# Routing each head in its own span of gather slots, five w_q kept for both tiles, nine row buffers and a 4 KB descriptor ring

## The chip, the cores and the metric

One core of one Trainium2 chip runs the whole program. The metric is the device time of one execution in microseconds; 1544.36 us is the median of three runs of the kernel before.

## The reference

A decoder trunk of two layers over 256 tokens with 1024 channels, all in float32. Each layer mixes tokens with four parallel head groups and then applies a PEER feed-forward, which looks up experts by product keys:

```python
for l in range(DEPTH):                                    # DEPTH = 2
    proj = x @ w_in[l]                                    # 1024 -> 2208 columns
    mix  = concat[short conv, MLA, conformer conv, windowed attention](proj)
    mix  = rms_norm per 64-channel head
    h    = layer_norm(ALPHA * x + mix @ w_out[l])
    x    = layer_norm(ALPHA * h + peer_ffn(h))

def chunk(xc):                                            # 128 tokens
    q  = (xc @ w_q).reshape(c, 8 heads, 2, 128)
    sc = einsum(q, sub_keys)                              # 2 x 128 scores a head
    top_s, top_i = top_k(sc, 16)                          # of each half
    best = top_k(sums of all 16 x 16 pairs, 16)           # 16 experts a head
    u, v = u_tab[idx], v_tab[idx]                         # 8 x 16 rows of 1024 each
    act  = gelu(einsum(u, xc))
    return einsum(softmax gate * act, v)
```

So each token reads 128 rows of u and of v per layer, and these rows are most of the traffic.

## The kernel before

The 256 tokens are two tiles of 128 (t = 0, 1), one token to a partition. With two layers there are four pairs (l, t), worked through in the order (0,0), (0,1), (1,0), (1,1).

**The gather loop.** `peer(l, t, h, acc)` makes 128 slots per pair, 512 in all. One slot is: an indirect DMA issued by POOL (L756) brings one expert's u and v for each of 128 tokens into a buffer `row` (128 x 2048 float32, 1.05 MB); DVE multiplies the u half by h and sums it (L759); ACT makes the gelu, the gate and a diagonal matrix `dg` (L741, L742, L744); PE adds `dg` times the v half into two PSUM banks `acc` (L746). The pool `gp` has `ROWS` = 10 buffers `row`, so a gather can be issued when PE has finished with the gather ten slots earlier.

**The routing.** `route(l, hd, hTs)` gives the indices of one head: it loads the head's weights `w_q` (1.18 MB, `load_w` on SP's queue), makes q and the scores on PE (L675, L680), and finds the two top-16 lists and the expert numbers on DVE (L632 to L658). With both tiles in `hTs` it serves both from one load. Heads 0 to 4 (`HS` = 5) are routed tile by tile, in `solo`; heads 5 to 7 for both tiles together, in `joint`. Of the first five, heads 0, 1 and 2 (`HELD`) keep `w_q` in buffers of their own (pool `rp`) until the second tile has used it; heads 3 and 4 load it a second time. Other weights (`w_in` pieces, `w_out`, remaining `w_q`) share three buffers `w` (pool `wp`).

**The mixer.** `mixer(l, t, ...)` makes h of a pair: nine pieces of `w_in`, two attentions, two convolutions, then `outs`, which multiplies by four loads of `w_out` (L586), one for each head group. h of (0,0) must be ready before the first gather; the other three mixers run beside the gathers of the pair before them.

**The order of work.** Routing and mixers are Python generators that yield a cost now and then. `paced(gather, tasks)` emits one slot of gathers, then advances each task `(generator, a, b, cost)` so that it is done evenly between slots a and b. Dependencies without semaphores (`keep_behind`) hold this work near its slot. Each engine and SP's DMA queue then run their instructions in the order in which they were emitted and scheduled. Before, `main_loop` gave, in slots of the pair whose gathers run:

| gathers of | tasks beside them (slots) |
|---|---|
| (0,0) | head 1 (0-4), heads 2-4 of (0,0) (4-17), mixer (0,1) (0-65), `joint(0)` (65-100) |
| (0,1) | heads 0-4 of (0,1) (2-36), mixer (1,0) (36-104), heads 0-1 of (1,0) (104-120) |
| (1,0) | heads 2-4 of (1,0) (3-17), mixer (1,1) (4-66), `joint(1)` (66-101) |
| (1,1) | heads 0-4 of (1,1) (2-70) |

The second tile uses its heads in the order 5, 6, 7, 0 to 4.

Of the kernel before, what the change touches and what calls it, by code (L numbers as in the profile page):

```python
# [61 lines left out]
def kernel(ctx: ExitStack, tc: tile.TileContext, x, positions, w_in, w_att, bcast, perch, lnrows, lncols,  # L62
# [223 lines left out]
    def mixer(l, t, y, xt):  # L286
# [65 lines left out]
        def group(g):  # L352
# [94 lines left out]
        def swa():  # L447
            ps = yield from proj_chunks(2, "swq")
            sq = mp.tile([P, 2, P], F32, tag="sq", name="sq")
# [41 lines left out]
        def conv_taps():  # L491
            cv2 = mp.tile([P, 2, P], F32, tag="ct", name="cv")
            cv = [cv2[:, j, :] for j in range(2)]
            for k in range(31):
                for j in range(2):
# [473 lines left out]
```

## Time and profile before

| | before |
|---|---|
| median of three runs (lowest, highest) | 1544.36 us (1543.88, 1546.22) |
| the profiled execution, its own time | 1543.23 us |
| its span, first to last instruction | 1541.2 us |
| mean granted TensorE clock | 0.975 of full speed |
| bytes moved by DMA, mean rate over the span | 614.47 MB, 399 GB/s |
| PE, DVE, ACT, POOL busy | 87%, 71%, 38%, 40% of the span |

The profile comes from one execution. An engine's busy share is over the whole span and hides that stretches of the program have different limits. A DMA share near 1.0 means that the DMA engines had packets at all times, and GB/s what these moved.

### The profile page before, as it was taken

The numbers are of one execution on the slowest core, as the hardware profiler recorded it, in microseconds if no ns is written. First come the engines' busy times: TensorE is split into PE (matmuls) and PEld (weight loads), VectorE is DVE, ScalarE is ACT, GpSimd is POOL, SyncE is SP. The second block draws the span as 40 slices with busy tenths as digits, with TensorE's granted clock in tenths as the row PEclk, the third lists the DMA queues.
The fourth block names the chain that finished last, engine by engine and source line by source line (L and its number), as shares of the span: only waits on it lengthen the run. The fifth ranks groups of instructions, "written<-read, shape, count | busy, mean of one in ns | idle before, by whom it ended". The sixth has DMA issues, their size and how long they took to land.

```text
span 1541.2 us, 17548 instructions
## 1 busy us (share of the span) xinstructions
PE 1345.3 (87%) x4868; PEld 720.2 (47%) x4868; DVE 1096.8 (71%) x3163; ACT 589.6 (38%) x2047; POOL 618.4 (40%) x539
## 2 busy tenths in 40 slices
PE   8999889798989789978989999898988898888776
PEld 8676444454335455533444665444543444432222
DVE  6789785699659775677487787757984777665445
ACT  4234442343434333354243334423443343433332
POOL 2044233234654233434335334232445454555551
PEclk9999899999999999999999999899999999999999
DMA  9579999999999999999999999999999999999995
GB/s 381 195 319 421 418 393 401 416 385 405 420 421 422 422 422 423 422 422 384 424 381 422 422 423 422 378 420 363 374 396 422 421 422 421 421 421 422 421 421 239
DMA packets 86209, 614.47 MB, mean 399 GB/s; under 512 B 10337, under 2 KB 10721, under 8 KB 12769
## 3 DMA queue, kind: packets, MB, share of 16 engines
q0 software_dynamic: 73728, 536.90, 84.9%
q1 hardware_dynamic: 12096, 76.44, 12.1%
q8 instruction: 40, 0.66, 0.2%
q14 instruction: 57, 0.46, 0.1%
q10 hardware_dynamic: 288, 0.01, 0.0%
HBM read 612.26 MB, written 1.05 MB: 398 GB/s over the span
## 4 chain that ended last, share of the span: by engine, by line
PE 39%; DMA 28%; DVE 22%; issue 6%; ACT 4%; POOL 0%; DVEq 0%; SPq 0%; POOLq 0%
DMA row<-in_uv_dram,ix 27%; PE acc L746 26%; DVE row L759 9%; PE ps_q L675 5%; PE ps_o L586 3%; DVE cv L510 1%; DMA w_in_t<-in_w_in_dram 1%; ACT dg L744 1%; PE ps_mla L320 1%; DVE bj L655 1%; DVE rsc L656 1%; DVE ti L655 1%; DVE grid L656 1%; DVE ti L658 1%; ACT act L742 1%
## 5 line engine op out<-in xcount | busy, mean ns | idle before, releaser
L746 PE MATMUL acc<-row,dg 128*128 128x512 f32 x2048 | 987.2, 615 | 162.0 <-ACT dg L744 160.8
L756 POOL DMA_INDIRECT row<-in_uv_dram,ix x512 | 607.4, 1186 | 866.0 <-PE acc L746 299.4
L759 DVE SCALAR_TENSOR_TENSOR row<-row,h 128x1024 f32<-128x1024 f32 x512 | 619.2, 1219 | 225.8 <-DMA row<-in_uv_dram,ix 201.2
L746 PEld LDWEIGHTS acc<-row,dg 128*128 128x128 f32 x2048 | 366.1, 193 | 643.7 <-ACT dg L744 331.9
L741 ACT ACTIVATE act<-act 128x1 f32<-128x1 f32 x512 | 103.1, 201 | 581.5 <-DVE row L759 580.7
L744 ACT ACTIVATE dg<-idn,act 128x128 f32<-128x128 f32 x512 | 205.1, 401 | 72.5 <-PE acc L746 58.5
L742 ACT ACTIVATE act<-act,gate 128x1 f32<-128x1 f32 x512 | 150.2, 294 | 15.5
L675 PEld LDWEIGHTS ps_q<-hT,w_q_t 128*128 128x128 f32 x1024 | 124.6, 194 | 23.3 <-issue 22.2
L675 PE MATMUL ps_q<-hT,w_q_t 128*128 128x128 f32 x1024 | 128.6, 278 | 5.8 <-DVE hp L153 5.6
L510 DVE SCALAR_TENSOR_TENSOR cv<-cfu,pc,cv 128x128 f32<-128x128 f32 x217 | 68.7, 358 | 0.9
L586 PE MATMUL ps_o<-w_out_t,mT 128*128 128x512 f32 x128 | 61.7, 615 | 1.7 <-DVE mT L370 1.7
L654 DVE MAX8 tv<-rsc 128x8 f32<-128x128 f32 x64 | 18.4, 289 | 46.8 <-ACT rsc L682 46.5
L682 ACT COPY rsc<-ps_rs 128x128 f32<-128x128 f32 x64 | 17.0, 265 | 66.7 <-PE ps_rs L680 66.4
L759 DVE DVE_READ_ACCUMULATOR row<-row,h 128x1 f32 x512 | 41.9, 82 | 0.0
L586 PEld LDWEIGHTS ps_o<-w_out_t,mT 128*128 128x128 f32 x128 | 24.7, 198 | 31.2 <-issue 28.7
L680 PEld LDWEIGHTS ps_rs<-w_q_t,rq 128*128 128x128 f32 x128 | 23.6, 190 | 29.4 <-issue 22.2
L592 DVE SCALAR_TENSOR_TENSOR hp<-x,ps_o 128x512 f32<-128x512 f32 x8 | 5.5, 687 | 38.5 <-PE ps_o L586 38.5
L678 ACT COPY rq<-ps_q 128x128 f32<-128x128 f32 x64 | 16.8, 262 | 39.7 <-PE ps_q L675 39.5
L680 PE MATMUL ps_rs<-w_q_t,rq 128*128 128x128 f32 x128 | 25.1, 278 | 2.1 <-ACT rq L678 2.1
L320 PEld LDWEIGHTS ps_mla<-w_in_t,xT 128*128 128x128 f32 x128 | 23.4, 196 | 4.0 <-issue 2.9
L320 PE MATMUL ps_mla<-w_in_t,xT 128*128 128x208 f32 x128 | 24.9, 348 | 0.2 <-DMA w_in_t<-in_w_in_dram 0.2
L649 DVE TENSOR_REDUCE ex<-grid 128x32 f32<-128x512 f32 (+1 forms) x33 | 22.0, 667 | 0.3
(215 smaller groups left out, 977.9 us busy)
## 6 DMA issues: line engine op xcount, KB each, us to landing
w_in_t<-in_w_in_dram SPq DMA_DIRECT2D x24, 1024.0 KB, 10.1
w_q_t<-in_w_qk_dram SPq DMA_DIRECT2D x20, 1152.0 KB, 9.4
w_out_t<-in_w_out_dram SPq DMA_DIRECT2D x16, 1024.0 KB, 10.4
row<-in_uv_dram,ix POOLq DMA_INDIRECT x512, 16.5
w_in_t<-in_w_in_dram SPq DMA_DIRECT2D x6, 832.0 KB, 7.9
att<-in_w_att_dram SPq DMA_DIRECT2D x2, 640.0 KB, 12.7
x<-in_x_dram SPq DMA_DIRECT2D x2, 512.0 KB, 6.7
gb<-in_lnrows_dram SPq DMA_DIRECT2D x1, 1024.0 KB, 13.6
```

What stands on the lines that cost most here:

```text
L320: nc.tensor.matmul(ps, xT[:, c, :], w[:, c, a:b], start=(c == 0), stop=(c == KC - 1))
L510: V.scalar_tensor_tensor(cv[j], src, wt, cv[j], op0=ALU.mult, op1=ALU.add)
L586: nc.tensor.matmul(po[j], mixed_T()[:, 2 * g + c, :], wg[:, c, j * 512:(j + 1) * 512], start=(n == 0 and c == 0), stop=(n == 3 and c == 1))
L655: V.max_index(idx[:, 0:8], val[:, 0:8], s)
L675: nc.tensor.matmul(ps, wq[:, c, j * P:(j + 1) * P], hT[:, c, :], start=(c == 0), stop=(c == KC - 1))
L680: nc.tensor.matmul(ps, qT, w[:, KC * 256 + j * P:KC * 256 + (j + 1) * P], start=True, stop=True)
L741: S.activation(act, act, AF.Gelu)
L742: S.activation(act, act, AF.Copy, scale=gate[:, k % TOPK:k % TOPK + 1])
L744: S.activation(dg, idn, AF.Copy, scale=act)
L746: nc.tensor.matmul(acc[j], dg, row[:, DM + j * 512:DM + (j + 1) * 512], start=(k == 0), stop=(k == n - 1))
L756: nc.gpsimd.indirect_dma_start(out=row, out_offset=None, in_=uv, in_offset=bass.IndirectOffsetOnAxis(ap=ix[:, k % TOPK:k % TOPK + 1], axis=0))
L759: V.scalar_tensor_tensor(row[:, :DM], row[:, :DM], 1.0, h, op0=ALU.mult, op1=ALU.mult, accum_out=act)
```

## The change

- Heads 0 to 4 all keep `w_q` for the second tile (`HELD`, five buffers of pool `rp`); heads 5 to 7 (`KEPT`) keep theirs in the three `w` buffers from the first tile's routing to the second's. Each `w_q` is loaded once a layer.
- `route` serves one head of one tile; `solo` and `joint` are gone. Each head gets a span of slots of its own. The mixers get longer spans: slots 0 or 3 to 80, and 3 to 98 for mixer (1,0).
- `ROWS` is 9. In the three mixers beside gathers, the four `w_out` loads go into `row` buffers instead of `w` buffers. `outs` yields after each matmul pair instead of each bank.
- Small tiles share buffers: `gsq` with `cT`, `pes` with `scc`, `sq` with `sg`, `tap` with `dg`; transposed tiles share tag `T` with two buffers. Two waits on `hot["pT"]` in the attentions are gone.
- The descriptor area of POOL's DMAs is set to 4096 bytes a partition; it was left at its default, 16384.

```diff
-ROWS = 10
+ROWS = 9
-HS = 5
+HELD = (0, 1, 2, 3, 4)
+KEPT = (5, 6, 7)
+HEADS = ((0, 1, 2, 3, 4, 5, 6, 7), (5, 6, 7, 0, 1, 2, 3, 4))
-MIX, ROUTE, TAIL = 97.0, 10.9, 6.6
+MIX, ROUTE, TAIL = 111.0, 10.9, 6.6
...
-            sq = mp.tile([P, 256], F32, tag="gsq", name="gsq")
+            sq = mp.tile([P, 256], F32, tag="cT", name="gsq")
...
                 if not start:
-                    wo[g] = w_out_rows(g)
+                    wo[g] = w_out_rows(g, gp.tile([P, 2 * DM], F32, tag="row", name="w_out_t"))
...
+                        if c == 0:
+                            yield 1.7
...
-    def route(l, hd, hTs):
+    def route(l, t, hd):
         n = QK
-        if hd in HELD and 1 in hTs:
-            w = held.pop(hd)
-        else:
+        w = held.pop((l, hd), None)
+        if w is None:
             if hd in HELD:
-                held[hd] = rp.tile([P, n], F32, tag=f"held{hd}", name="w_q_t")
-            w = load_w(w_qk, (l * NH + hd) * P * n, n, "w_q_t", held.get(hd))
+                w = rp.tile([P, n], F32, tag=f"held{hd}", name="w_q_t")
+            w = load_w(w_qk, (l * NH + hd) * P * n, n, "w_q_t", w)
+            if t == 0 and hd in HELD + KEPT:
+                held[l, hd] = w
...
+    def routes(l, t, spans):
+        return [(route(l, t, hd), a, b, ROUTE) for hd, (a, b) in spans.items()]
...
+            tasks = [(tail, 0, 3, TAIL)] if i else []
+            if t == 0:
+                tasks += routes(l, 0, {1: (0, 3)} if l == 0 else {})
+                tasks += routes(l, 0, {2: (0, 17), 3: (17, 32), 4: (32, 48), 5: (48, 64), 6: (64, 80)})
+                tasks += [(mix(1, 1) if l else ahead, 0 if l == 0 else 3, 80, MIX)]
+                tasks += routes(l, 1, {5: (80, 94)}) + routes(l, 0, {7: (84, 97)}) + routes(l, 1, {6: (97, 112), 7: (112, 128)})
             else:
-                tasks = [(tail, 0, 3, TAIL), (solo(1, 1, range(HS)), 2, 70, HS * ROUTE)]
+                tasks += routes(l, 1, {0: (3, 20), 1: (20, 38), 2: (38, 56), 3: (56, 74), 4: (74, 92)})
+                if l == 0:
+                    tasks += [(mix(1, 0), 3, 98, MIX)] + routes(1, 0, {0: (98, 112), 1: (112, 126)})
...
-    nc = _bacc.Bacc("TRN2", target_bir_lowering=False, num_devices=1)
+    nc = _bacc.Bacc("TRN2", target_bir_lowering=False, num_devices=1, dynamic_dma_scratch_size=4096)
```

The scheduler makes an order out of this. Three places of it follow, before and after, with the buffers' numbers; line numbers of the new kernel are three to five higher or lower for the same statement.

SP's DMA queue ahead of the first gather, before: `gb` and the loads after it. `w_q` 823, 931, 1088, 1235 and 1394 are heads 0, 1, 2, 3 and 4 of layer 0; `w_in` 1405, 1441 and 1713 are pieces of mixer (0,1). Names in brackets are semaphores waited for; DMAHW ones are those of earlier loads, PE and DVE ones those of a buffer's last reader.

```order
L605 DMA gb_751<-in_lnrows_dram 128x2048 [waits DMAHW1_49]
L162 DMA w_q_t_823<-in_w_qk_dram 128x2304 [waits DMAHW2_49]
L162 DMA w_q_t_1235<-in_w_qk_dram 128x2304 [waits DMAHW6_49,DMAHW3_49,PE_49]
L162 DMA w_q_t_1394<-in_w_qk_dram 128x2304 [waits DMAHW7_49,DMAHW4_49,PE_49]
L162 DMA w_q_t_1088<-in_w_qk_dram 128x2304 [waits DMAHW5_49,DVE_49,PE_49]
L162 DMA w_in_t_1405<-in_w_in_dram 128x2048 [waits DMAHW0_49]
L162 DMA w_q_t_931<-in_w_qk_dram 128x2304 [waits DMAHW1_49,DVE_49]
L162 DMA w_in_t_1441<-in_w_in_dram 128x2048 [waits DMAHW3_49,PE_49]
L162 DMA w_in_t_1713<-in_w_in_dram 128x2048 [waits DMAHW6_49,PE_49]
```

The same place after. Here 810, 931, 957, 1409 and 1770 are heads 0 to 4, 2190 and 2487 heads 5 and 6; 1300, 1331 and 1628 the pieces of mixer (0,1); `w_out` 134 is that of the head group that mixer (0,0) multiplies first.

```order
L606 DMA gb_751<-in_lnrows_dram 128x2048 [waits DMAHW0_49]
L165 DMA w_q_t_810<-in_w_qk_dram 128x2304 [waits DMAHW1_49]
L165 DMA w_q_t_1409<-in_w_qk_dram 128x2304 [waits DMAHW2_49]
L165 DMA w_q_t_1770<-in_w_qk_dram 128x2304 [waits DMAHW3_49]
L165 DMA w_out_t_134<-in_w_out_dram 128x2048 [waits DMAHW4_49,PE_49]
L165 DMA w_in_t_1300<-in_w_in_dram 128x2048 [waits DMAHW5_49,PE_49]
L165 DMA w_in_t_1331<-in_w_in_dram 128x2048 [waits DMAHW6_49,PE_49]
L165 DMA w_q_t_957<-in_w_qk_dram 128x2304 [waits DMAHW7_49,DVE_49,PE_49]
L165 DMA w_in_t_1628<-in_w_in_dram 128x2048 [waits DMAHW0_49]
L165 DMA w_q_t_931<-in_w_qk_dram 128x2304 [waits DMAHW1_49,DVE_49]
L165 DMA w_q_t_2190<-in_w_qk_dram 128x2304 [waits DMAHW5_49,DMAHW2_49,PE_49]
L165 DMA w_q_t_2487<-in_w_qk_dram 128x2304 [waits DMAHW6_49,DMAHW3_49,PE_49]
```

Heads 3 and 4 go without a wait for PE, `w_out` 134, before ahead of the other three `w_out`, has moved behind them, `gb` and three `w_q` and waits for PE, and all three pieces of `w_in` stand ahead of head 1, two of them ahead of head 2.

PE's queue at the end of mixer (0,0), before. `ps_mT` is the transpose of one head group's output, `ps_o` the product with `w_out`, `ps_xT` the start of mixer (0,1).

```order
L369 MATMUL ps_mT_645<-idn_88,m_540 128x128 x2
L586 MATMUL ps_o_664<-w_out_t_134,mT_648 128x512 x2
L586 MATMUL ps_o_704<-w_out_t_134,mT_648 128x512 x2
L369 MATMUL ps_mT_723<-idn_88,m_638 128x128 x2
L586 MATMUL ps_o_664<-w_out_t_185,mT_648 128x512 x2
L586 MATMUL ps_o_704<-w_out_t_185,mT_648 128x512 x2
L369 MATMUL ps_mT_727<-idn_88,m_643 128x128 x2
L369 MATMUL ps_mT_733<-idn_88,m_652 128x128 x2
L586 MATMUL ps_o_664<-w_out_t_187,mT_648 128x512 x2
L586 MATMUL ps_o_704<-w_out_t_187,mT_648 128x512 x2
L122 MATMUL ps_xT_754<-idn_88,x1_91 128x128 x4
L586 MATMUL ps_o_664<-w_out_t_189,mT_648 128x512 x2
```

The same place after.

```order
L372 MATMUL ps_mT_645<-idn_88,m_540 128x128 x2
L372 MATMUL ps_mT_720<-idn_88,m_638 128x128 x2
L372 MATMUL ps_mT_724<-idn_88,m_643 128x128 x2
L585 MATMUL ps_o_664<-w_out_t_134,mT_648 128x512 x2
L585 MATMUL ps_o_728<-w_out_t_134,mT_648 128x512 x2
L585 MATMUL ps_o_664<-w_out_t_185,mT_648 128x512 x2
L585 MATMUL ps_o_728<-w_out_t_185,mT_648 128x512 x2
L585 MATMUL ps_o_664<-w_out_t_187,mT_648 128x512 x2
L372 MATMUL ps_mT_730<-idn_88,m_652 128x128 x2
L585 MATMUL ps_o_728<-w_out_t_187,mT_648 128x512 x2
L125 MATMUL ps_xT_754<-idn_88,x1_91 128x128 x4
L585 MATMUL ps_o_664<-w_out_t_189,mT_648 128x512 x2
```

The transposes of the second and third group now stand ahead of the first `ps_o`.

SP's DMA queue between layer 0's routing of heads 5 to 7 and mixer (1,0), before: `w_q` 2509, 2775 and 3041 are heads 5 to 7, 4097 and 4246 the second load of heads 3 and 4, `w_in` 4436 the first piece of mixer (1,0).

```order
L162 DMA w_q_t_2509<-in_w_qk_dram 128x2304 [waits DMAHW3_49,PE_49]
L162 DMA w_q_t_2775<-in_w_qk_dram 128x2304 [waits DMAHW5_49,PE_49]
L162 DMA w_q_t_3041<-in_w_qk_dram 128x2304 [waits DMAHW7_49,PE_49]
L162 DMA w_q_t_4097<-in_w_qk_dram 128x2304 [waits DMAHW4_49,DMAHW1_49,PE_49]
L162 DMA w_q_t_4246<-in_w_qk_dram 128x2304 [waits DMAHW2_49,PE_49]
L162 DMA w_in_t_4436<-in_w_in_dram 128x1664 [waits DMAHW6_49,DMAHW3_49,PE_49]
```

The same place after: 2858 is head 7, the four `w_out` are those of mixer (0,1), 3713 the first piece of mixer (1,0). DMASW semaphores are those of gathers.

```order
L165 DMA w_q_t_2858<-in_w_qk_dram 128x2304 [waits DMAHW0_49,PE_49]
L214 DMA bc_3673<-in_bcast_dram 128x900 [waits DVE_49]
L165 DMA w_out_t_2296<-in_w_out_dram 128x2048 [waits DMASW2_49,DMASW3_49,DMASW1_49,DMASW4_49,DMASW0_49,DMAHW7_49,DVE_49,PE_49]
L214 DMA pc_3674<-in_perch_dram 128x78 [waits DVE_49,Activation_49]
L165 DMA w_out_t_2381<-in_w_out_dram 128x2048 [waits DMASW2_49,DMASW6_49,DMASW1_49,DMASW7_49,DMASW0_49,DMAHW1_49,DVE_49,PE_49]
L165 DMA w_out_t_2438<-in_w_out_dram 128x2048 [waits DMASW6_49,DMASW5_49,DMAHW2_49,DVE_49,PE_49]
L165 DMA w_out_t_2526<-in_w_out_dram 128x2048 [waits DMASW4_49,DMASW3_49,DMAHW3_49,DVE_49,PE_49]
L165 DMA w_in_t_3713<-in_w_in_dram 128x1664 [waits DMAHW4_49,PE_49]
```

The two second loads are gone, and the `w_out` loads wait for gathers and for their readers on DVE and PE.

## Rows read from the trace of the kernel before

**Rows 1.** The profile's page: span and DMA packets.
```profile
span 1541.2 us, 17548 instructions
...
DMA packets 86209, 614.47 MB, mean 399 GB/s; under 512 B 10337, under 2 KB 10721, under 8 KB 12769
```

**Rows 2.** Busy time by stretch (x: instructions), granted clock, DMA share, GB/s.
```profile
core 0: us, PE busy (x) PEld busy (x) DVE busy (x) ACT busy (x) POOL busy (x), PEclk, DMA share, GB/s
0.00:100.00 100.00, 89.58 (x580) 74.83 (x581) 67.89 (x288) 33.38 (x95) 19.73 (x35) 0.97 0.71 280
...
220.00:250.00 30.00, 28.74 (x85) 13.86 (x84) 22.59 (x61) 11.94 (x41) 12.16 (x11) 0.99 0.96 360
...
300.00:360.00 60.00, 53.26 (x228) 31.49 (x227) 54.56 (x180) 25.80 (x101) 22.23 (x21) 1.00 0.97 383
...
700.00:730.00 30.00, 26.04 (x67) 11.66 (x68) 23.03 (x64) 16.27 (x51) 12.90 (x11) 0.94 0.96 373
...
780.00:810.00 30.00, 24.81 (x82) 11.95 (x82) 27.61 (x84) 12.32 (x48) 11.18 (x11) 1.00 0.97 370
810.00:980.00 170.00, 157.24 (x678) 97.34 (x677) 133.59 (x406) 71.17 (x242) 69.03 (x57) 0.97 1.01 422
980.00:1010.00 30.00, 30.00 (x86) 14.48 (x85) 20.43 (x56) 12.38 (x39) 10.64 (x10) 0.91 0.92 361
...
1050.00:1160.00 110.00, 96.02 (x347) 51.09 (x348) 95.55 (x298) 46.77 (x180) 45.49 (x41) 1.00 0.97 375
1160.00:1520.00 360.00, 300.91 (x791) 124.69 (x790) 222.87 (x491) 135.79 (x475) 183.22 (x141) 1.00 1.01 421
1520.00:1541.20 21.20, 9.49 (x20) 3.09 (x18) 11.85 (x27) 3.59 (x12) 0.00 (x0) 0.85 0.23 92
```

**Rows 3.** The page's DMA queues (packets, MB, share) and issues (median us to landing).
```profile
q0 software_dynamic: 73728, 536.90, 84.9%
...
w_in_t<-in_w_in_dram SPq DMA_DIRECT2D x24, 1024.0 KB, 10.1
w_q_t<-in_w_qk_dram SPq DMA_DIRECT2D x20, 1152.0 KB, 9.4
...
row<-in_uv_dram,ix POOLq DMA_INDIRECT x512, 16.5
```

**Rows 4.** Timeline of 51 to 94 us: start, us, engine, line, operation.
```profile
52.16 6.08 PE L586 MATMUL ps_o<-w_out_t,mT 128*128 128x512 f32 x8 [0.52 <-DVE mT L370]
...
55.88 0.16 DVE L108 SCALAR_TENSOR_TENSOR rs_y<-rs_u,rs_y 128x4 f32<-128x4 f32 x1
...
59.31 3.70 PE L586 MATMUL ps_o<-w_out_t,mT 128*128 128x512 f32 x8 [0.85 <-DVE mT L370]
...
67.72 3.60 PE L586 MATMUL ps_o<-w_out_t,mT 128*128 128x512 f32 x8
...
87.81 1.08 POOL L756 DMA_INDIRECT row<-in_uv_dram,ix  x1 [51.86 <-issue]
```

**Rows 5.** Busy time by stretch, 50 to 60 us.
```profile
50.00:60.00 10.00, 8.63 (x20) 4.22 (x20) 6.92 (x39) 1.93 (x5) 0.00 (x0) 0.66 0.00 1
```

**Rows 6.** Chain that ended last: the first gather it passes through (start, us).
```profile
87.81 5.66 DMA row<-in_uv_dram,ix
```

**Rows 7.** POOL's waits over the whole span: total us, times, longest us.
```profile
POOL row L756 <- PE acc L746: 299.4, 150, 19.0
...
POOL row L756 <- PE ps_rs L680: 89.4, 44, 6.0
```

**Rows 8.** POOL's longest waits in 970 to 1010 us.
```profile
POOL row L756 <- PE acc L746: 19.4, 7, 9.6
```

**Rows 9.** POOL's longest waits in 1045 to 1140 us.
```profile
POOL row L756 <- PE ps_rs L680: 23.4, 10, 2.8
```

**Rows 10.** DVE's two groups of a gather: busy us, mean ns, idle before.
```profile
L759 DVE SCALAR_TENSOR_TENSOR row<-row,h 128x1024 f32<-128x1024 f32 x512 | 619.2, 1219 | 225.8 <-DMA row<-in_uv_dram,ix 201.2 <-ACT dg L744 18.2 <-ACT act L741 2.8
...
L759 DVE DVE_READ_ACCUMULATOR row<-row,h 128x1 f32 x512 | 41.9, 82 | 0.0
```

More of the change, by code (lines that the diff above doesn't have):

```diff
@@ L424, in mla @@
             yield from take("S")
-            while not start and hot["pT"]:
-                yield None
             yield from take("m", 2)
@@ L463, in swa @@
             yield from take("S")
-            while not start and hot["pT"]:
-                yield None
             yield from take("m", 2)
@@ L731 @@
-    R, held = {}, {}
-    HELD = (0, 1, 2)
+        if (l, t) not in HT:
+            HT[l, t] = transpose8(H[l, t], f"hT{t}")
+            yield 1.5
+        hT = HT[l, t]
+        s = []
+        for j in range(2):
+            ps = pm.tile([P, P], F32, tag="mm", name="ps_q")
+            for c in range(KC):
+                nc.tensor.matmul(ps, wq[:, c, j * P:(j + 1) * P], hT[:, c, :], start=(c == 0), stop=(c == KC - 1))
+            yield 1.8
+            qT = sp.tile([P, P], F32, tag=f"rq{j}", name="rq", bufs=1)
+            S.copy(qT, ps)
+            ps = pm.tile([P, P], F32, tag="mm", name="ps_rs")
+            nc.tensor.matmul(ps, qT, w[:, KC * 256 + j * P:KC * 256 + (j + 1) * P], start=True, stop=True)
+            s.append(sp.tile([P, P], F32, tag=f"rsc{j}", name="rsc", bufs=1))
+            S.copy(s[j], ps)
+            yield 0.3
@@ new lines, in route @@
+        tv = sp.tile([P, 2, TOPK], F32, **(dict(tag="ex0", bufs=1) if (l, t) == (0, 0) and hd < KEPT[0] else dict(tag="tv")),
+                     name="tv")
+        ti = sp.tile([P, 2, TOPK], U32, tag="ti", name="ti")
+        for j in range(2):
+            top16(tv[:, j, :], ti[:, j, :], s[j])
+            yield 1.0
+        top16(bs, bj, sum_grid(tv, TOPK))
+        yield 2.0
+        ix = gp.tile([P, TOPK], I32, tag=f"ix{hd}", name="ix", bufs=2)
+        experts(l, ix, bj, ti, TOPK, TOPK)
@@ L734, in peer @@
+        sm = sp.tile([P, 1], F32, tag="gsm", name="gsm")
+        gate = gp.tile([P, TOPK], F32, tag=f"gate{hd}", name="gate", bufs=2)
+        S.activation(tm, tm, AF.Square)
+        S.activation(tm, tm, AF.Square)
+        S.activation(gate, tm, AF.Square, accum_out=sm)
+        V.reciprocal(sm, sm)
+        V.tensor_scalar(gate, gate, sm, None, op0=ALU.mult)
+        R[l, t, hd] = (ix8, ix, gate)
+        yield 0.5
+    R, held, HT = {}, {}, {}
     def peer(l, t, h, acc):
         n = NH * TOPK
-        order = list(range(HS, NH)) + list(range(HS)) if t else list(range(NH))
+        order = HEADS[t]
@@ L778 @@
     H = {}
-    hot = dict(pT=0)
     def mix(l, t):
@@ L785, in mix @@
         H[l, t] = yield from mixer(l, t, Y[l], X[t])
-    def solo(l, t, heads):
-        if t == 0 and not hot["pT"]:
-            hot["pT"] = transpose8(H[l, 0], "hT0", "pT")
-            yield 1.5
-        for hd in heads:
-            yield from route(l, hd, {t: hot["T"] if t else hot["pT"]})
-        if t == 0 and hd == HS - 1:
-            hot["pT"] = 0
-    def joint(l):
-        hot["T"] = transpose8(H[l, 1], "hT1", "T")
-        yield 1.5
-        hT0 = transpose8(H[l, 0], "hT0", "pT")
-        yield 1.5
-        for hd in range(HS, NH):
-            yield from route(l, hd, {0: hT0, 1: hot["T"]})
     log = nc.cur_bb.bb.instructions
@@ L862 @@
                 next(ahead)
-    for _ in solo(0, 0, [0]):
+    for _ in route(0, 0, 0):
         pass
+    def routes(l, t, spans):
+        return [(route(l, t, hd), a, b, ROUTE) for hd, (a, b) in spans.items()]
     def main_loop():
```

102 lines of the change are left out of this document (30 added, 72 removed).

## Prediction

> **What bounds the kernel now.** I read the busy time by stretch first [rows 2], then POOL's waits [rows 7 to 9], then the start as a timeline [rows 4]. From 1160 to 1520 us the DMA engines are busy throughout and move 421 GB/s, in 810 to 980 us 422. I take 422 GB/s for the rate at which DMA is the limit. All 614.47 MB [rows 1] at that rate take 1456 us; the span is 1541.2, so 85 us are lost, and the stretches below the rate show where. Each loses its length times (1 - rate/422):
>
> - 0 to 100 us: 33.6 us. The mixer of (0,0) must end before the first gather goes at 87.8 us [rows 4].
> - 1520 us to the end: 16.6 us, for the last gathers' arithmetic and the last layer norm.
> - 300 to 360 and 1050 to 1160 us: 5.5 + 12.2 = 17.7 us. This is `joint`: DVE is busy 91% and 87%, and POOL's gathers wait behind the scores' matmul `ps_rs`, 23.4 us in ten waits [rows 9].
> - 220 to 250, 700 to 730 and 980 to 1010 us: 4.4 + 3.5 + 4.3 = 12.2 us. These are the ends of the three mixers beside gathers, where `w_out` is multiplied; POOL waits for `acc`, that is for PE to free a row buffer [rows 8].
> - 780 to 810 us: 3.7 us, where heads 0 and 1 of (1,0) are routed.
>
> These make 83.8; the rest is rounding. So a load less in a stretch at 422 saves its whole time, an instruction less on DVE or PE saves time only in the slow stretches. PE's and DVE's averages say nothing of this.
>
> **The loads removed.** 20 `w_q` loads of 1152 KB [rows 3] become 16. Four times 1.18 MB at 422 GB/s is 11.2 us. Two are the second loads of heads 3 and 4 for (0,1), shown in the order of SP's queue; two are those for (1,1), which fall into 1160 to 1520 us. Both places are at the full rate, nothing else waits there, so I count -11.2. If PE or DVE limited those stretches it would be 0; DVE is busy only 62% of the last one.
>
> **The start.** The order of PE moves the first `ps_o` behind the transposes of two more groups. The third of the three needs DVE's last step for it, which could start when `rs_y` ends at 55.9 + 0.2 us [rows 4], takes 0.4, and the transposes some 0.3: `ps_o` begins near 56.8 instead of 52.2. Before, its four groups took 6.1, 3.7, 3.7 and 3.6 us, the first slow because the granted clock was at its lower level, 1.2 GHz (mean 0.66 of full in 50 to 60 us [rows 5]), after PE had been waiting for the attention's steps; the last ended at 71.3. After, four groups at 3.7 and a microsecond of transposes end at 72.6, or at 75.0 if the first again takes 6.1. So the first gather goes 1.3 to 3.7 us later. I take +3, since PE now waits longer ahead of `ps_o`. A rule speaks for the late end: the Trainium skill (TensorE: Matmul & The Clock Gate, Part 1) says that an idle PE falls to half clock and returns to full only after it has been busy for some time. By it alone this term would be +3.7, with every group at full clock +1.3. The late `w_out` 134 costs nothing: two more `w_q` are 5.6 us of DMA, and DMA stood still from 50 to 60 us [rows 5]. If it did come late, each microsecond would count in full.
>
> The same queue now issues the three `w_in` pieces of mixer (0,1) ahead of the first gather, where before one went and two waited for PE until gathers ran. Two megabyte loads [rows 3] are 5.0 us of DMA, moved out of the full stretch into idle time: -5.0; 0 if they land among the first gathers. Start together: -2 (-3.7 to +3.7).
>
> **`joint` gone.** Before, it routed three heads for two tiles in 35 slots, 0.17 routes a slot. In 1050 to 1160 us 41 gathers were issued [rows 2], whose DVE work is 41 x (1.22 + 0.08) = 53 us [rows 10]; the other 42 us of DVE's 95.6 are some 7 routes, 6 us each. After, a span has about 16 slots for one route, twice as dense only in slots 84 to 94: 1.3 + 6/16 = 1.7 us of DVE a slot, against 2.49 us that a 1.05 MB gather takes of DMA. The mixer now has routes beside it throughout, 5 of them in slots 3 to 80. Its nearest row is 810 to 980 us, with mixer (1,1) and three heads: DVE 79% busy, and yet 422 GB/s. So of the 17.7 us I leave 3 for latencies: -14.7 (between -17.7 and -8, if half of the lost time is the latency of single routes). Heads 0 and 1 of (1,0) lie in 28 slots instead of 16: -1.7 of 3.7.
>
> **Fewer row buffers.** This goes against it. A buffer is held from a gather's issue until PE has used it. At the full rate ten buffers last 10 x 2.49 = 24.9 us; a gather lands 16.5 us after its issue [rows 3], so about 8 go to the arithmetic. With little queued, the first gather on the chain takes 5.7 us [rows 6]. The rest, some 11 us, is how long PE and DVE may lag before DMA runs dry; each buffer less makes that 2.49 us shorter. In the even stretches, nine suffice. In the built program, three stretches of some 22 slots reuse a buffer seven or eight gathers old, since one or two hold `w_out`. They are just the three where ten ran dry by 4 us each. The `w_out` transfers, 2.5 us each, keep DMA busy in part. Bounds: if each lost buffer (2 to 2.5 of them) shows in full, 3 x 2.5 x 2.49 = +18.7; if the finer steps of `outs` remove PE's backlog, -12.2. I take half the upper bound, +9, because rows 8 show POOL already waiting for PE here. In other stretches +2 (0 to +8) for stalls that ten buffers covered. What is queued behind a waiting gather on POOL is only the next gather; behind a `w_out` that waits on SP stand loads needed tens of slots later.
>
> The shared small tiles change the start mixer's order nowhere else that I could find; beside the gathers a wait of a microsecond on `cT` or `sg` is covered by the eleven microseconds above. Cover gone, it counts in full.
>
> **Sum.** 1541.2 - 11.2 - 2 - 14.7 - 1.7 + 9 + 2 = 1522.6 us of span. The execution's own time stood 2.0 us above its span (1543.2), the median another 1.1: 1525.7. The spread of ends is wider below than above, so I forecast 1524 us.
>
> **Rivals.**
>
> 1. *The ring takes back what `joint` gave.* All three `w_out` stretches pay +18.7, other stalls +4, and `joint` gives only 8: 1541.2 - 11.2 - 2 - 8 - 1.7 + 18.7 + 4 = 1541, or 1544 as a median; half way to it 1535. For it: 150 waits of POOL on `acc`, 299 us [rows 7]. Against: most of them are the ring's normal wait while DMA is full.
> 2. *Slower: PE's lag empties the short ring each time.* If every longer wait for `acc`, not only those in the three stretches, now empties the queue, each lost buffer costs 2.49 us a time. The gains above are 29.6 us without ring losses; twelve dry spells of one buffer use them up, 16 make 1541.2 - 29.6 + 40 = 1551, with the 3.1 us 1554. The place is slots 40 to 80 of each mixer, where PE waits for softmax chains.
> 3. *Larger gain.* `outs` in finer steps keeps PE's backlog down, the three stretches lose nothing, and all of `joint` goes: 1541.2 - 11.2 - 2 - 17.7 - 3.7 - 12 = 1494.6, with 3.1 1498; half way 1509.
> 4. *The small descriptor area limits gathers in flight.* The larger one held at least 16.5/2.49 = 6.6 gathers; a quarter of it might hold only 1.7. At 5.7 us each that is 3.4 us a slot instead of 2.49, over 512 slots +460 us. It decides below 5.7/2.49 = 2.3 in flight. Against: a gather makes 73728/512/16 = 9 packets an engine [rows 3], not many. The Trainium skill (DMA: Bandwidth & Descriptors, Terms) gives a descriptor as 16 bytes; by it 4096 bytes would hold 256, an estimate of 28 gathers, and nothing would change. No run here shows it yet.
>
> **Chances.** The forecast, 1515 to 1535: 0.50. Rival 3, 1498 to 1515: 0.20. Rival 1, 1535 to 1547: 0.19. Rivals 2 and 4, above: 0.08 and 0.03. Two thirds of what lies below 1515 are above 1504, so the range is 1504 to 1545; it leaves 0.07 below, and above it 0.11 of rivals 2 and 4 and some 0.02 of rival 1, which is denser at its lower end. Its own range for the forecast is 1515 to 1535. A measurement tells this kernel from no change at about 0.2%, 3.1 us: faster means below 1541.3. From rival 1 two thirds are faster: 0.50 + 0.20 + 0.13 = 0.83; the same 0.06; slower 0.11.
>
> **What would show it.** Sixteen `w_q` issues and 609.8 MB; the first gather near 90.8 us; no stretch of tens of microseconds below 400 GB/s after the mixers, where POOL waited for `ps_rs`; dips at the ends of the mixers as deep as before or deeper, with POOL waiting for `acc`; gathers that land about 14 us after issue, not 16.5. I would be wrong if the start's mixer ends much later, if the dips stay where `joint` was, or if the ends of the mixers lose more than 10 us each.

## The result and the profile after

The changed kernel takes 1525.34 us (median of four runs, 1523.25 to 1527.36) against 1544.12 beside it: ratio 0.9877, 95% interval 0.986 to 0.9894, 18.8 us less. The forecast was 1524. The total was right, two of its large terms were not, and a term that was missing made up for them.

The page of the changed kernel: span, packets, `w_q` loads.

```profile
span 1523.7 us, 17524 instructions
...
DMA packets 85632, 609.75 MB, mean 400 GB/s; under 512 B 10272, under 2 KB 10656, under 8 KB 12704
...
w_q_t<-in_w_qk_dram SPq DMA_DIRECT2D x16, 1152.0 KB
```

Its busy time by stretch, columns as in [rows 2]. The last four rows cut the span where DVE starts on the first gather of each pair, and end where it starts on the last gather of all.

```profile
220.00:250.00 30.00, 28.11 (x106) 15.61 (x106) 23.11 (x79) 12.42 (x45) 9.51 (x9) 0.94 0.88 327
...
300.00:360.00 60.00, 53.58 (x192) 28.03 (x190) 47.51 (x140) 21.20 (x77) 23.59 (x24) 1.00 0.99 400
...
640.00:680.00 40.00, 33.84 (x92) 15.77 (x91) 28.08 (x90) 12.99 (x47) 14.57 (x11) 0.90 0.93 358
...
700.00:730.00 30.00, 26.99 (x61) 10.88 (x59) 15.45 (x32) 8.42 (x30) 11.27 (x12) 1.00 1.01 427
...
780.00:810.00 30.00, 25.40 (x57) 9.59 (x56) 22.82 (x62) 11.93 (x43) 14.76 (x13) 1.00 1.01 426
...
940.00:1000.00 60.00, 50.15 (x184) 27.54 (x184) 51.61 (x182) 30.22 (x94) 20.36 (x17) 0.94 0.88 326
...
1050.00:1160.00 110.00, 101.13 (x354) 53.03 (x353) 84.41 (x236) 43.38 (x166) 49.78 (x46) 1.00 1.01 418
1160.00:1500.00 340.00, 287.79 (x764) 120.54 (x763) 221.26 (x504) 131.00 (x459) 147.28 (x135) 1.00 1.01 427
...
95.50:455.70 360.20, 322.55 (x1180) 173.78 (x1179) 280.17 (x850) 146.41 (x521) 150.17 (x132) 0.99 0.99 408
455.70:822.10 366.40, 326.98 (x1185) 176.49 (x1184) 265.51 (x747) 142.69 (x496) 144.54 (x127) 0.98 1.00 419
822.10:1192.40 370.30, 331.35 (x1250) 182.83 (x1251) 279.85 (x824) 146.90 (x516) 144.86 (x129) 0.99 0.98 401
1192.40:1509.10 316.70, 266.41 (x705) 111.17 (x706) 203.43 (x458) 121.68 (x426) 130.91 (x121) 1.00 1.00 420
```

Of the kernel before, at 640 us:

```profile
640.00:680.00 40.00, 29.56 (x93) 14.13 (x91) 27.72 (x85) 19.15 (x54) 15.83 (x12) 0.91 1.01 421
```

Three things are to be seen. Where `joint` was, DMA is nearer its limit (400 and 418 GB/s against 383 and 375 in [rows 2]), and at 780 us, where [rows 2] has the two heads of (1,0), it is at it (426 against 370). The dips in the mixers are deeper, and one is new. In mixer (0,1), 220 to 250 us move 327 GB/s, 360 before. Mixer (1,0) had its dip in 700 to 730 us, beside the exponentials of an attention (`S_mla`, 701 us); now these run at 634 us and the dip stands in 640 to 680: 40 x (1 - 358/427) = 6.5 us are lost, 3.5 before. In mixer (1,1), 14.2 us are lost in 940 to 1000, where [rows 2] has 422 GB/s up to 980. And the limit itself is another: DMA, busy all the time, moves 427 GB/s in the last stretch and not 421. On the 536.9 MB of gathers alone that is some 18 us, about the whole gain, and nothing in the prediction speaks of it.

### The profile page after: what moved, and what is told of

It is laid out like the page before. It is cut to its first block, busy times and chain, and to the rows that moved or that the text cites. A ratio compares the mean times of both kernels' runs of the same rounds, so it can differ in the third digit from the quotient of the medians.

```text
span 1523.7 us, 17524 instructions
## 1 busy us (share of the span) xinstructions
PE 1334.1 (88%) x4852; PEld 714.4 (47%) x4852; DVE 1098.6 (72%) x3161; ACT 588.5 (39%) x2047; POOL 586.1 (38%) x539
## 2 busy tenths in 40 slices
DMA packets 85632, 609.75 MB, mean 400 GB/s; under 512 B 10272, under 2 KB 10656, under 8 KB 12704
## 3 DMA queue, kind: packets, MB, share of 16 engines
q1 hardware_dynamic: 11520, 71.72, 11.5%
## 4 chain that ended last, share of the span: by engine, by line
PE 40%; DMA 26%; DVE 22%; ACT 6%; issue 4%; POOL 1%; DVEq 0%; SPq 0%; POOLq 0%; ACTq 0%
DMA row<-in_uv_dram,ix 25%; PE acc L750 24%; DVE row L763 10%; PE ps_q L680 5%; PE ps_o L585 3%; DVE cv L509 2%; ACT dg L748 2%; PE ps_mla L323 2%; POOL row L760 1%; ACT act L746 1%; PE ps_cfa L319 1%; PE ps_cfg L319 1%; ACT act L745 1%; PE ps_rs L685 1%; ACT L745 1%
## 5 line engine op out<-in xcount | busy, mean ns | idle before, releaser
L760 POOL DMA_INDIRECT row<-in_uv_dram,ix x512 | 575.0, 1123 | 883.3 <-PE acc L750 390.2
L585 PE MATMUL ps_o<-w_out_t,mT 128*128 128x512 f32 x128 | 59.5, 608 | 0.0
L683 ACT COPY rq<-ps_q 128x128 f32<-128x128 f32 x64 | 16.4, 256 | 53.8 <-PE ps_q L680 53.0
L649 DVE TENSOR_TENSOR grid<-tf,ab 128x512 f32<-128x512 f32 (+1 forms) x33 | 22.3, 674 | 0.7
```

The lines of the kernel that those rows point to most:

```text
L760: nc.gpsimd.indirect_dma_start(out=row, out_offset=None, in_=uv, in_offset=bass.IndirectOffsetOnAxis(ap=ix[:, k % TOPK:k % TOPK + 1], axis=0))
```

## Experiments

Ratios are to the kernel before, timed on the same chip; a difference of two ratios times 1544 us is the price between two kernels.

### What raised the rate: the descriptor area, or fewer gathers in flight?

The kernel before, with one line of the change each. The descriptor area first:

```diff
-    nc = _bacc.Bacc("TRN2", target_bir_lowering=False, num_devices=1)
+    nc = _bacc.Bacc("TRN2", target_bir_lowering=False, num_devices=1, dynamic_dma_scratch_size=4096)
```

> The kernel before, with only the descriptor area set to 4096 bytes. The changed kernel moves 427 GB/s where DMA is the limit, the kernel before 422. If the smaller descriptor area is the cause: 427 GB/s in the last hundreds of us, and 614.47 MB x (1/422 - 1/427) = 17 us less, about 1527 us. If the nine row buffers (fewer gathers in flight) are the cause: 422 GB/s as before, 1544 us, within 3.

Then a row buffer less:

```diff
-ROWS = 10
+ROWS = 9
```

> The kernel before, with only nine row buffers instead of ten. If fewer gathers in flight raise the rate: 427 GB/s late in the span, -17 us, and against it what a shorter ring loses in the mixers, +5 to +15: about 1532 to 1542 us. If the descriptor area raises the rate: 422 GB/s and only the ring's loss, 1547 to 1560 us, with dips in the middle of the mixers where the kernel before has none.

Measured: 1543.95 us, ratio 0.9995 (0.9985 to 1.0004), and 1545.33 us, 0.9998 (0.9989 to 1.0008). Both move 421 GB/s in 1200 to 1480 us, as the kernel before. Neither is the cause. The descriptor area costs and gives nothing that can be measured (rival 4 is gone), and in the kernel before a buffer less costs nothing either.

### The address of the row buffers

The changed kernel and its two variants of the next part all move 427 GB/s, with nine, eight and ten buffers. What they share is where the rows begin in a partition: at byte 149248 or 140032, a multiple of 256. Those with 421 have them at 142720 or 130432, 128 bytes behind one. So one small tile, which lies ahead of them in memory, was made longer: in the kernel before by 128 bytes, in the changed one by 128 (as here) and by 224 (`[P, 64]`). All that lies behind it moves along.

```diff
-b8 = sp.tile([P, 8], F32, tag="b8", name="b8", bufs=1)
+b8 = sp.tile([P, 40], F32, tag="b8", name="b8", bufs=1)[:, :8]
```

> The kernel before, with one small tile made 128 bytes longer, so that its ten row buffers begin at a multiple of 256 bytes in a partition, as in the changed kernel, instead of 128 bytes behind one. Nothing else differs. The three kernels with 427 GB/s so far (the changed one, eight buffers, ten buffers with four heads kept) have rows at multiples of 256, the three with 421 (before, before with the small descriptor area, before with nine buffers) 128 bytes behind one. If the address is the cause: 427 GB/s late in the span and 1525 to 1530 us. If it is a coincidence: 421 GB/s and 1544 us. The Trainium skill (DMA: Bandwidth & Descriptors, How a descriptor splits into AXI transactions) says that a descriptor which does not start at a multiple of 256 bytes pays for the bytes from the multiple below it; by that, 8192 bytes at an offset of 128 take 260 beats instead of 256, 1.6% on the gathers.

> The changed kernel with its rows moved by 128 bytes, to where the kernel before has them. If the address is the cause of the rate: 421 GB/s, and where DMA is the limit 609.75 MB x (1/421.5 - 1/427) = 18.6 us more, less what the slow stretches hide: 1538 to 1544 us, so that all the rest of the change gave nearly nothing. If not: 427 GB/s and 1525 us.

> The changed kernel with its rows moved by 224 bytes. If any address off a multiple of 256 costs the same: 421 GB/s and the time of the 128-byte shift, 1538 to 1544 us. If the cost grows with the distance from the multiple below: more than that, some 417 GB/s and 1550 to 1560 us. The Trainium skill's account of the split (DMA: Bandwidth & Descriptors, How a descriptor splits into AXI transactions) gives 263 beats instead of 256 for a gather's 8192 bytes, 2.7%, an estimate of 417 GB/s over all.

Late stretch of the three, in this order (columns as in [rows 2]):

```profile
1200.00:1480.00 280.00, 236.36 (x646) 101.32 (x646) 184.49 (x429) 108.42 (x383) 147.44 (x113) 1.00 1.01 427
```

```profile
1200.00:1480.00 280.00, 234.95 (x640) 100.17 (x640) 183.44 (x426) 107.03 (x378) 119.94 (x111) 1.00 1.01 421
```

```profile
1200.00:1480.00 280.00, 233.50 (x637) 99.72 (x638) 182.71 (x425) 106.53 (x376) 115.94 (x111) 1.00 1.01 420
```

| kernel | rows begin, past a multiple of 256 | us | ratio (interval) |
|---|---|---|---|
| before, rows moved | 0 | 1534.51 | 0.9935 (0.9917 to 0.9953) |
| changed | 0 | 1525.34 | 0.9877 (0.986 to 0.9894) |
| changed, rows moved by 128 | 128 | 1537.99 | 0.9962 (0.9948 to 0.9976) |
| changed, rows moved by 224 | 224 | 1539.59 | 0.9964 (0.9953 to 0.9976) |

The rate follows the address both ways, with no other edit: 10 us in the kernel before, where 14 to 19 were expected, and 13 in the changed one. That it is the rows, and not another of the tiles that moved, shows in the DMA records of the traces: in 1200 to 1480 us the median 8192-byte packet of a gather takes 309 ns with rows at a multiple of 256, 313 with 128 and with 224; in 450 to 600 us that of the 8192-byte loads from SP's queue, which go mostly into buffers `w` that the longer tile does not move, takes 309 in all five kernels. Of the 18.8 us more than half comes from 128 bytes by which the reshuffled small tiles happened to move the rows. A shift of 224 costs little more than one of 128 (420 against 421 GB/s); a price that grows with the distance is not seen.

### Each head in its own span

The changed kernel with the spans of the kernel before (the last pair has 2 to 36 for its five heads here, not 2 to 70).

```diff
...
-tasks += routes(l, 0, {2: (0, 17), 3: (17, 32), 4: (32, 48), 5: (48, 64), 6: (64, 80)})
-tasks += [(mix(1, 1) if l else ahead, 0 if l == 0 else 3, 80, MIX)]
-tasks += routes(l, 1, {5: (80, 94)}) + routes(l, 0, {7: (84, 97)}) + routes(l, 1, {6: (97, 112), 7: (112, 128)})
+tasks += routes(l, 0, {2: (4, 8), 3: (8, 13), 4: (13, 17)})
+tasks += [(mix(1, 1) if l else ahead, 4 if l else 0, 66 if l else 65, MIX)]
+for j, hd in enumerate(KEPT):
+    tasks += routes(l, 0, {hd: (66 + 12 * j, 72 + 12 * j)}) + routes(l, 1, {hd: (72 + 12 * j, 78 + 12 * j)})
...
-tasks += routes(l, 1, {0: (3, 20), 1: (20, 38), 2: (38, 56), 3: (56, 74), 4: (74, 92)})
+tasks += routes(l, 1, {0: (2, 9), 1: (9, 16), 2: (16, 23), 3: (23, 30), 4: (30, 36)})
...
-    tasks += [(mix(1, 0), 3, 98, MIX)] + routes(1, 0, {0: (98, 112), 1: (112, 126)})
+    tasks += [(mix(1, 0), 36, 104, MIX)] + routes(1, 0, {0: (104, 112), 1: (112, 120)})
```

> The changed kernel with the spans of slots of the kernel before: heads 2 to 4 in slots 4 to 17, the mixers in slots 0 or 4 to 66 and 36 to 104, heads 5 to 7 of both tiles densely in 66 to 102, heads 0 and 1 of (1,0) in 104 to 120. By the prediction: the dense routing comes back with 14.7 us, the two heads with 1.7, so 1540 to 1543 us. The rival after the two traces: the wider spans only moved the loss, since the changed kernel has new dips in the middle of the mixers (640 to 680 and 940 to 1000 us, some 20 us) where routes now run beside them; then these vanish as the dense ones return, and the time stays within 6 us of 1525.

Measured: 1536.49 us, 0.9943 (0.992 to 0.9966), 10.2 us more than the changed kernel. The four pairs, cut as above:

```profile
96.30:462.00 365.70, 326.54 (x1179) 174.79 (x1179) 278.57 (x844) 146.08 (x520) 142.62 (x132) 0.98 0.97 402
462.00:826.60 364.60, 319.40 (x1166) 170.94 (x1167) 263.55 (x751) 144.53 (x495) 138.25 (x127) 0.99 1.01 421
826.60:1203.70 377.10, 336.84 (x1270) 185.39 (x1269) 280.38 (x825) 150.97 (x517) 140.62 (x130) 0.99 0.96 393
1203.70:1521.30 317.60, 265.94 (x705) 110.27 (x705) 199.37 (x458) 121.94 (x426) 127.29 (x121) 1.00 1.00 419
```

The loss is in the pairs where `joint` was: +5.5 us in the first and +6.8 in the third, +0.9 in the last. The second pair, with the two heads of (1,0), is 1.8 shorter with the old spans. The spans gave some 10 us, six tenths of the 16.4 forecast. A little of it isn't the old spans' doing: the last pair, with its heads in half the slots, dips to 368 GB/s in 1280 to 1300 us, where the kernel before has none. The rival in the expectation falls too: the dip of mixer (1,1) stays with the old spans (238 and 228 GB/s in 940 to 960 and 960 to 980 us), with no route beside the mixer there, so the wider spans didn't make it.

The kernel before with its rows moved has the same address and the same spans up to the last pair. Its pairs:

```profile
95.00:460.40 365.40, 326.50 (x1188) 175.44 (x1187) 278.38 (x846) 146.24 (x521) 152.41 (x132) 0.97 1.00 409
460.40:825.10 364.70, 323.14 (x1153) 174.61 (x1154) 264.03 (x752) 141.22 (x494) 145.40 (x126) 0.97 1.01 419
825.10:1203.20 378.10, 341.21 (x1292) 188.87 (x1291) 280.95 (x825) 147.95 (x517) 152.96 (x130) 0.98 0.99 405
1203.20:1519.00 315.80, 265.41 (x705) 111.21 (x706) 202.83 (x459) 121.33 (x426) 158.31 (x120) 1.00 1.00 422
```

They are within 2 us of those above, 1424.0 us together against 1425.0. So beside the address and the spans, all the rest of the change (four loads fewer, the shorter ring with `w_out` in it, the finer steps, the shared tiles) gives nothing in the loop, taken together.

### Loads and buffers

Four kernels around the changed one. The first has a buffer less. The second and third keep four heads and load the fifth's `w_q` twice, without and with a tenth row. The fourth puts the memory of the fifth head into a fourth buffer `w` and loads `w_out` there.

```diff
-ROWS = 9
+ROWS = 8
```

> The changed kernel with eight row buffers instead of nine. If the ring's length sets the depth of the dips (one gather, 2.46 us, for each dry spell): the changed kernel has some ten stretches of 20 us below 400 GB/s, so +10 to +25 us, 1535 to 1550 us, with the dips at the same places but deeper. If the dips come from the density of work on PE and DVE whatever the ring: within 4 us of 1525. If fewer gathers in flight raise the rate, it is over 430 GB/s late in the span; else 427.

```diff
-HELD = (0, 1, 2, 3, 4)
+HELD = (0, 1, 2, 3)
```

> The changed kernel, which keeps four heads' w_q instead of five and loads head 4 twice a layer: two more loads, nine row buffers as before. By the prediction's price a load on the path costs its bytes at the full rate: 2.36 MB at 427 GB/s, +5.5 us, 1531 us; then the tenth buffer of the kernel with ten rows and four heads (1521.4 us) is worth 9.5 us, as the ninth was over the eighth (9.3). Rival: loads are hidden and cost nothing, 1525 us, and the tenth buffer is worth 4.

As this one, with `ROWS = 10`:

> The changed kernel with ten row buffers, paid for in memory by keeping four heads' w_q instead of five: head 4 is loaded twice a layer, two more loads, 2.36 MB at 427 GB/s = +5.5 us. If the ninth-to-tenth buffer is what the dips in the middle of the mixers lack: these lose 2.5 us less in some six spells, -10 to -15, in sum 1515 to 1521 us. If they don't depend on it: 1531 us. If ten buffers bring the rate back to 422 GB/s: 16 us more than either.

As a_held4, with these two lines:

```diff
-wp = ctx.enter_context(tc.tile_pool(name="wp", bufs=3))
+wp = ctx.enter_context(tc.tile_pool(name="wp", bufs=4))
...
-wo[g] = w_out_rows(g, gp.tile([P, 2 * DM], F32, tag="row", name="w_out_t"))
+wo[g] = w_out_rows(g)
```

> As the kernel with four heads kept and nine rows, but with the memory of the fifth head as a fourth buffer w, and w_out loaded into these buffers again and not into row buffers. By the prediction, w_out in the ring costs 9 us in three stretches: 9 us less than that kernel, some 1522 us. If it costs little, since its transfers keep DMA busy in part: within 3 us of that kernel, some 1531 us.

| kernel | us | ratio (interval) | first gather at, us | the four pairs, us |
|---|---|---|---|---|
| changed | 1525.34 | 0.9877 (0.986 to 0.9894) | 89.8 | 360.2, 366.4, 370.3, 316.7 |
| eight rows | 1534.67 | 0.9926 (0.991 to 0.9943) | 99.4 | 367.2, 364.8, 365.4, 316.9 |
| four heads kept | 1524.35 | 0.9868 (0.9852 to 0.9885) | 91.8 | 360.5, 364.8, 370.6, 316.2 |
| four heads, ten rows | 1521.36 | 0.9845 (0.9829 to 0.9861) | 87.9 | 356.3, 363.6, 375.2, 317.0 |
| four heads, `w_out` in `w` | 1518.58 | 0.9830 (0.9813 to 0.9848) | 91.9 | 355.5, 367.2, 365.8, 317.0 |

- **Two loads more cost nothing that can be measured** (-1.4 us, with the intervals overlapping), where +5.5 us was expected. The first and third pair of the kernel with four heads:

```profile
97.30:457.80 360.50, 323.26 (x1183) 173.97 (x1182) 280.49 (x850) 145.84 (x520) 147.63 (x132) 0.99 1.00 411
...
822.60:1193.20 370.60, 333.65 (x1250) 183.30 (x1250) 280.83 (x824) 147.90 (x516) 144.05 (x129) 0.99 0.99 408
```

  The third pair has two loads more in it, one of them moved there from the second pair, and one goes at 936 us into the dip (372 GB/s in 940 to 960 us instead of 287). So it moves 408 GB/s instead of 401 in the same 370 us: this pair is not paced by its bytes.

- **The ring's length matters ahead of the loop, and not in the sum of it.** Eight rows: +9.6 us until the first gather, +0.7 over the four pairs. Ten, against four heads with nine: -3.9 until the first gather, 0.0 over the pairs. In these sums two effects cancel: the ninth and the tenth buffer make the first pair shorter (by 7.0 and 4.2 us) and the third longer (by 4.9 and 4.6). Why the third gets longer stays open. The row buffers also take the pieces of `w_in` and one `w_out` of the first mixer. With eight of them PE waits 8.64 us for a piece of `w_in`. Timelines of the first mixer and the first gather, with eight rows and then with ten:

```profile
51.44 5.19 PE L319 MATMUL ps_sch<-xT,w_in_t 128*128 128x128 f32 x32 [8.64 <-DMA w_in_t<-in_w_in_dram]
...
65.92 3.70 PE L585 MATMUL ps_o<-w_out_t,mT 128*128 128x512 f32 x8 [0.62 <-DVE mT L373]
...
99.36 1.09 POOL L760 DMA_INDIRECT row<-in_uv_dram,ix  x1 [63.30 <-issue]
```

```profile
52.11 6.24 PE L585 MATMUL ps_o<-w_out_t,mT 128*128 128x512 f32 x8 [0.52 <-DVE mT L373]
...
87.92 1.08 POOL L760 DMA_INDIRECT row<-in_uv_dram,ix  x1 [52.07 <-issue]
```

- **`w_out` in the ring costs 5.9 us** (0.9868 - 0.9830): 5.0 in the first pair, 4.8 in the third, and a gain of 2.4 in the second. The kernel without it has a fourth buffer `w` as well; the two weren't told apart.

### Towards a better kernel

Both with ten rows, and `outs` in the coarser steps at the start. The first keeps four heads and gives mixer (1,1) the order of parts of layer 0:

```diff
-if c == 0:
+if c == 0 and not start:
...
-yield from sequence(SEQ1 if l == 0 else SEQ, chains)
+yield from sequence(SEQ1 if l == 0 or t else SEQ, chains)
```

> Ten rows and four heads kept (1521.4 us), with two edits more: at the start `outs` yields by bank again as in the kernel before, and mixer (1,1) takes its parts in the order of layer 0 (attentions before convolutions), since 940 to 1040 us of the kernel with ten rows lose 23 us and the same stretch of mixer (0,1) only 7. If the finer steps made the start late, the first gather goes at 87.8 us instead of 89.8: -2. If the order is what makes the dip in (1,1): -8 to -16. Together 1503 to 1511 us. Rival: the dip comes from the routes beside the mixer, and the order only shifts it: 1517 to 1522 us.

The second keeps three heads, leaves the order of parts alone, and has `w_out` in four buffers `w`, by the two lines of a_held4_wp4:

```diff
...
-HELD = (0, 1, 2, 3, 4)
+HELD = (0, 1, 2)
```

> The kernel with w_out in four buffers w (1518.6 us, first gather at 91.9 us) with three edits more: ten rows, paid for by keeping only heads 0 to 2 (two more loads, 2.36 MB), and at the start `outs` yields by bank again. The row buffers also take w_in and w_out of the first mixer; the first gather went at 99.4, 91.8 and 87.9 us with eight, nine and ten rows, and at 84.9 with ten rows and the coarser steps. So the start gives 7 us; the tenth row gave 4 us in pair 0; if loads beside the mixers are hidden, as the first two more of them were, 1508 to 1512 us; if they now count in full, +5.5: 1513 to 1517.

Measured: 1523.46 us, 0.9867 (0.9847 to 0.9887), and 1518.99 us, 0.9838 (0.9825 to 0.9851). Both lie above the ranges expected, that of the rival in the first (1517 to 1522 us) and that for loads that count in full in the second (1513 to 1517) included. The first gather goes at 84.9 and 85.0 us, where 87.8 was expected of the first. `ps_o` starts at 51.6 us, and every group runs in 3.7, at the full granted clock (1.00 of 2.4 GHz from 51.6 to 56 us in both). The coarser steps alone don't explain that: the kernel before has them too, and its first group takes 6.1 [rows 4]. The order of parts made the third pair of the first one 3.5 us longer, not shorter (378.7 against 375.2, with ten rows and four heads). The second is no better than the kernel with four heads and `w_out` in `w`: its six runs spread from 1512.59 to 1520.88, and its profiled one is the lowest, so its pairs aren't read here. Both kernels with `w_out` in `w` are 6 to 7 us faster than the changed one.

## Why the prediction was right, point by point

- **The rate.** The step that failed most: "422 GB/s for the rate at which DMA is the limit" was taken for both kernels. It is 427 with rows at a multiple of 256 bytes; shown, 10 to 13 us. The place of a buffer in memory was looked at for no term. The Trainium skill (DMA: Bandwidth & Descriptors, How a descriptor splits into AXI transactions) has a rule that bears on it: a descriptor that doesn't start at a multiple of 256 bytes also fetches the bytes from the multiple below, and pays for them. Counted out by it, an estimate, that is 1.6% for 8192 bytes at 128 and 2.7% at 224. In the late stretch, where nearly all bytes are gathers', the rows show 1.4% and 1.7%: the trace agrees on the direction and about on the first size, not on the growth.
- **The loads, -11.2.** The four went (609.75 MB), but "both places are at the full rate" misread where they were. The four second loads in SP's queue of the kernel before, issue by issue:

```profile
317.10 0.33 SPq L162 DMA_DIRECT2D w_q_t<-in_w_qk_dram  x1
...
350.18 0.33 SPq L162 DMA_DIRECT2D w_q_t<-in_w_qk_dram  x1
...
1065.90 0.33 SPq L162 DMA_DIRECT2D w_q_t<-in_w_qk_dram  x1
...
1102.06 0.33 SPq L162 DMA_DIRECT2D w_q_t<-in_w_qk_dram  x1
```

  None falls into 1160 to 1520 us. All four lie in the stretches of `joint`, at 383 and 375 GB/s, where POOL waits for `ps_rs`; "nothing else waits there" was wrong too. In the changed kernel two such loads put back cost -1.4 us instead of +5.5, so at least for these the term was too large. What the other two are worth alone wasn't tried.
- **`joint` and the two heads, -16.4.** For `joint` right in mechanism and place; 10.2 in size for both, and the -1.7 of the two heads isn't seen, since the second pair got 1.8 us longer by the wide spans. POOL's wait behind `ps_rs` in 1045 to 1140 us fell from 23.4 us [rows 9] to 4.3:

```profile
POOL row L760 <- PE acc L750: 28.3, 20, 2.8
...
POOL row L760 <- PE ps_rs L685: 4.3, 4, 2.1
```

- **The start, -2.** The step by DVE's third group and PE's order came true: `ps_o` starts at 56.9 us (56.8 forecast), the first gather goes at 89.8 (90.8). Changed kernel, timeline from 54 us:

```profile
55.88 0.42 DVE L368 TENSOR_TENSOR m<-m,rs_y 128x256 f32<-128x256 f32 x1
56.90 10.56 PE L585 MATMUL ps_o<-w_out_t,mT 128*128 128x512 f32 x20
...
69.67 3.60 PE L585 MATMUL ps_o<-w_out_t,mT 128*128 128x512 f32 x8
...
89.76 1.09 POOL L760 DMA_INDIRECT row<-in_uv_dram,ix  x1 [54.06 <-issue]
```

  And the busy time by stretch at the same place:

```profile
50.00:57.00 7.00, 2.35 (x12) 1.48 (x11) 6.26 (x37) 1.89 (x5) 0.00 (x0) 0.52 0.25 107
57.00:60.00 3.00, 3.00 (x5) 1.24 (x5) 2.52 (x14) 0.15 (x1) 0.00 (x0) 0.50 0.00 0
60.00:63.00 3.00, 3.00 (x7) 1.26 (x6) 0.67 (x3) 0.00 (x0) 0.00 (x0) 0.91 0.00 0
63.00:74.00 11.00, 11.00 (x36) 5.59 (x35) 2.50 (x4) 0.84 (x2) 0.00 (x0) 1.00 0.55 192
```

  PE, which was idle for two thirds of the 7 us ahead, runs `ps_o` at the lower granted clock, 1.2 GHz (0.50 of full), until some 60 us, and the last group ends at 73.3, between the two ends worked out (72.6 and 75.0). That is +2.0, inside the bounds of 1.3 and 3.7. One cause of the order was not seen: of the two kernels with four heads and the same fine steps, the one with nine rows starts `ps_o` at 59.5 us and the one with ten at 52.1. But the missing buffer doesn't do it alone: the kernel before with nine rows starts `ps_o` at 52.8 us and the first gather at 88.2. As for the -5, two pieces of `w_in` did move ahead of the first gather (26.0 MB have landed by then, 23.9 before); what that gave isn't shown.
- **The ring, +9 and +2.** `w_out` in the ring 5.9, with a fourth buffer `w` in the same edit; the rest of the ring about 0 over the loop, as the kernel before with nine rows and the sum of the pairs with eight show. The wait that a full ring adds fell with its length (DVE starts on a gather 17.5 us after its issue in the last pair, 19.2 before), as the step said, and with little to lose.
- **Together.** Address -11.5 (the mean of both sides), spans -10.2, `w_out` +5.9, start +2.0 make -13.8 of -18.8. The -5.0 that is left is for the four loads, the steps of `outs` beside gathers and the shared tiles; it isn't split, and since each of these prices is known to some 2 to 4 us, it isn't told from nothing. Without the luck of the address the change is worth 6 to 9 us (0.9962 with the rows moved, against the kernel before; 0.9877 against 0.9935 with both at a multiple of 256). That is less than half of the 20 forecast: 1537.99 us lies in the range of rival 1, 1535 to 1547. So the mechanism was right for `joint` and the start, and the total by luck.
- **Rival 2** had the right place: the dip beside mixer (1,1), at slots 40 to 61 of the gathers of (1,0), is new, and lies beside a softmax chain. But it doesn't follow the ring: with ten rows the third pair is longer, 375.2 us. The changed kernel at 940 us:

```profile
938.91 1.28 ACT L745 ACT_TABLE_LOAD   x1
940.20 0.20 ACT L745 ACTIVATE act<-act 128x1 f32<-128x1 f32 x1
...
940.75 1.28 ACT L269 ACT_TABLE_LOAD   x1
942.04 0.20 ACT L269 ACTIVATE es<-es 128x4 f32<-128x4 f32 x1
942.16 0.39 ACT L748 ACTIVATE dg<-idn,act 128x128 f32<-128x128 f32 x1
...
942.59 6.37 PE L750 MATMUL acc<-row,dg 128*128 128x512 f32 x8 [5.05 <-ACT dg L748]
942.87 1.28 ACT L745 ACT_TABLE_LOAD   x1
...
946.65 1.91 POOL L760 DMA_INDIRECT row<-in_uv_dram,ix  x1 [7.89 <-DVE cv L509]
```

  A gather's `gelu` falls between the two exponentials of the softmax; each change of function loads a table, 1.28 us, `dg` comes late, PE waits 5.05 us and then takes 6.37 for eight multiplications, at first at the lower granted clock (0.50 of full in 942 to 946 us, 1.2 GHz), and POOL waits 7.89. The kernel with ten rows has two table loads fewer in all and dips there too (279, 316 and 276 GB/s from 940 to 1000 us, 20 us each), so this is one way to the dip and not the cause of it. Neither the spans, nor the ring, nor the order of the parts, nor `w_out` back in `w` (394, 322 and 324 GB/s) removed it. The shared tiles, the finer steps beside gathers and the two waits taken out of the attentions were not undone alone; the waits held an attention back until the routing ahead of it was done, and are an untried rival. It stays open.

## What to carry to other kernels

Where DMA is the limit, look at the address of the buffers first: in this kernel 128 bytes were worth as much as the reorganisation of all routing, and any edit of an unrelated tile can shift them. Before a load is priced at the full rate, look up in the trace when it was issued: here all four lay in stretches below that rate, and two such loads put back into the changed kernel cost nothing. And count every user of a pool that shrinks: with eight rows the loop as a whole hardly noticed, and the start paid 9.6 us.

## What the hardware showed

- Gathers of 8192 bytes a partition move 427 GB/s into rows at a multiple of 256 bytes, 421 with rows 128 bytes behind one, 420 with 224. It is 427 with eight, nine and ten row buffers, and 421 with nine and ten.
- A descriptor area of 4096 bytes a partition instead of 16384 changes nothing that these runs can tell (0.9985 to 1.0004).
